# A transformer block's last stage: products in another order, operand sums made later, and all tokens written feature by feature

## The chip, the cores and the metric

The kernel runs on one core of one Trainium2 chip, in fp32 throughout. The metric is the device time of one execution in microseconds (us). Five engines work side by side, each through its own list of instructions in order: TensorE, shown as PE (matmuls) and PEld (loads of the stationary operand), VectorE (DVE), ScalarE (ACT), GpSimd (POOL) and SyncE (SP). DMAs are issued from an engine's list, here mostly SP's, and carried out by 16 DMA engines. An instruction that has to wait for another engine or for a transfer holds up everything behind it on its own engine.

## The reference

A block of a decoder with 1024 tokens and width 1024: a gated mixer of an mLSTM and of causal pools, then a SwiGLU layer of inner width 2816, then a last norm. The change touches the last two lines and nothing ahead of them.

```python
D_MODEL = 1024; SEQ = 1024; D_FF = 2816; EPS = 1e-6
def rms_norm(x, g):
    return x * lax.rsqrt(jnp.mean(x * x, axis=-1, keepdims=True) + EPS) * g
...
        x = x + (g_a * y_a + g_b * y_b) @ w_out[l]
        h2 = rms_norm(x, norm2_g[l])
        x = x + (jax.nn.silu(h2 @ w_ffn_gate[l]) * (h2 @ w_ffn_up[l])) @ w_ffn_down[l]
    return rms_norm(x, final_norm_g)
```

Inside the kernel most of it is held transposed: eight tiles of 128 features (`KT` = 8, `P` = 128), each with the tokens in a row.

## The kernel before, in words

**fp32 products.** A product of two fp32 blocks is three matmuls (`mm3`, lines 143 to 145): each operand is split into a high and a low part (`operand`, `split`: ACT casts the high part, line 131, DVE subtracts it for the low part, line 132), and high by high, high by low and low by high are summed in a PSUM bank of 128 x 512. `BANKS` gives 6 banks to "mm" and 2 to "aux".

**Seven products instead of eight.** The SwiGLU layer's last product, the *down stage*, treats the matrices as two by two blocks and gets the result from seven block products of sums, not eight. `OPS` names them b11, d1, d2, b21, d3, b22, d4. Their right operands (`tg`: hidden units by 512 tokens, high and low part side by side) were made in the gate/up stage ahead and lie in DRAM (`tg_d`). Their left operands (`a`) are made in the down stage from the four blocks of the weight: `a11`, `a12` (loaded into `raw`, `fh` = 0) and `a21`, `a22` (loaded into `rb`, `fh` = 1). b11 takes a11, b21 takes a12, d4 takes -a22; the other four take sums: s1 = a21 + a22 for d1, s1 - a11 for d2, a12 - (s1 - a11) for b22, a11 - a21 for d3.

**Loops.** The hidden units go in three chunks (`CHUNKS`: 4, 3 and 4 pairs of 128). In each chunk the seven steps of `STEPS` follow one another, and in each step the four column blocks `q` (`KH` = 4). One entry (c, s, q) is 12 matmuls of 512 columns (9 in the middle chunk) into one bank, and then DVE adds the bank to one half of a tile of `x` (the list `x3`, 8 tiles of 128 features x 1024 tokens, loaded at line 970 from the layer's input `x2_d`); this addition at line 1037 is called the eviction. In each half of the tiles are 512 tokens: the early ones (0 to 511) and the later ones.

**What is made ahead.** `down_rights` (line 938) queues a whole step's right operands on SP one step ahead; `tgp` has 13 places for them. `make_ready(e + EARLY)` makes the left operand of the entry four ahead. `down_lefts` is a generator that hands out a column's seven operands in the order of the steps; when d1's is asked for, it makes all four sums one after another (lines 920 to 924). The next chunk's weights are loaded in step three (`raw`) and step six (`rb`).

**Where the tiles lie.** The down stage's pools take the places that the gate/up stage's pools on the right side of SBUF had. In the order of their declaration (`s1p`, `rbp`, `tgp`, `ap`) they come to lie on that stage's operand tiles (in the trace `fb...`, `fd...`), and a first load into a place waits for the last matmul on the tile that lay there.

**The end.** In the last chunk finished features are squared and summed. The later 512 tokens are normed when d3 has come (`later_tokens`: a column of sums by four small matmuls, line 280; a power on POOL; the factor spread along a row by two matmuls on `diag`, line 273; one scaling for each of eight tiles, line 1004) and go out feature by feature as `out_0`. The early 512 tokens are turned into rows (`turn`: 28 transposes on PE, line 993, into `rows`), and the last entry runs in two halves of 256 tokens, each followed by its squares, its sum, its power, two transposes (line 1077), the scaling of whole rows by a number per partition (lines 1086 and 1088) and the output as `out_1` (line 1089).

The instructions on every engine are put in order by a scheduler that runs on a model of times, so the order in the program is not the code's.

Of the kernel before, what the change touches and what calls it, by code (L numbers as in the profile page):

```python
# [8 lines left out]
F32 = mybir.dt.float32  # L9
F32R = mybir.dt.float32r  # L10
# [37 lines left out]
EARLY = 4  # L48
# [18 lines left out]
def tile_hybrid_block(ctx, tc, x, xt, consts, params, w_fm, w_v, w_pool, w_a, w_b, w_out, w_gate, w_up, w_down, out, out_rows):  # L67
# [704 lines left out]
    with ExitStack() as c5:  # L772
# [121 lines left out]
        raws, lefts, rights, todo = {}, {}, {}, []  # L894
# [8 lines left out]
        def down_lefts(c, q):  # L903

            a11, a12 = raws[c, q, 0]
            n = a11.shape[-1]

            def tile_():
                t = ap.tile([P, 2, 512], F32R, tag="a", name="a")
                return t[:, :, :n]  # L910

            def op(src):
                t = tile_()
                operand(t, src)
# [5 lines left out]
            nc.vector.tensor_add(out=s1, in0=a21, in1=a22)  # L920
# [3 lines left out]
            nc.vector.tensor_sub(out=a12, in0=a12, in1=s1)  # L924
            yield t
            yield op(a12)
            yield op(a11)
            yield op(s1)
            yield op(a21)
            t = tile_()  # L930
            nc.scalar.activation(out=t[:, 0, :], in_=a22, func=AF.Copy, scale=-1.0)
            nc.vector.scalar_tensor_tensor(out=t[:, 1, :], in0=a22, scalar=-1.0, in1=t[:, 0, :].bitcast(F32), op0=ALU.mult, op1=ALU.subtract)
            yield t

        def down_rights(c, s):
            for i in range(*CHUNKS[c]):
                t = tgp.tile([P, 2, 512], F32R, tag="tg", name="tg")
                nc.sync.dma_start(out=t.bitcast(F32), in_=tg_d[i, OPS.index(STEPS[s])].rearrange("p (a n) -> p a n", a=2))
                rights.setdefault((c, s), []).append(t)

        entries = [(c, s, q) for c in range(len(CHUNKS)) for s in range(len(STEPS)) for q in range(KH)]

        def make_ready(e):
            if e >= len(entries):
                return
            c, s, q = entries[e]
            if s == 0:
                lefts[c, q] = down_lefts(c, q)
            todo.append(next(lefts[c, q]))
# [14 lines left out]
    op = pool(c7, "op", 4)  # L964
# [7 lines left out]
    rows = [op.tile([P, D], F32, tag="o", name="o") for _ in range(4)]  # L972
    LAST = KT - 1
    acc = [None, None]

    def square(j, half):

        sq = sqd.tile([P, 512], F32, tag=f"sq{half}", name="sq")
        nc.scalar.activation(out=sq, in_=halves(x3[j])[half], func=AF.Square)
        if acc[half] is not None:  # L980
            nc.vector.tensor_add(out=sq, in0=acc[half], in1=sq)
        acc[half] = sq

    def scaled(j):
        r = halves(x3[j])[0]
        nc.scalar.activation(out=r, in_=r, func=AF.Copy, scale=col(A_NF, j))

    def turn(t, j0, j1):

        ps = bank()  # L990
        n = (j1 - j0) * P
        for j in range(j0, j1):
            nc.tensor.transpose(out=ps[:, (j - j0) * P:(j - j0 + 1) * P], in_=x3[j][:, t * P:(t + 1) * P], identity=ident)  # L993
        copy = nc.scalar.copy if t % 2 else nc.vector.tensor_copy
        copy(out=rows[t][:, j0 * P:j1 * P], in_=ps[:, :n])

    def later_tokens():

        rs = sm.tile([P, 4], F32, tag="rs", name="rs3")
        inverse_rms(sm, token_sums(acc[1], 4), rs)  # L1000
        along_rows(sm, rsb2[0], rs, ap.tile([P, 2, 512], F32R, tag="a", name="diag"), 4)
        for j in range(KT):
            r = halves(x3[j])[1]
            nc.vector.scalar_tensor_tensor(out=r, in0=r, scalar=col(A_NF, j), in1=rsb2[0], op0=ALU.mult, op1=ALU.mult)  # L1004
            nc.sync.dma_start(out=out[j], in_=r)
# [5 lines left out]
    A, C = [None] * KH, [None] * KH  # L1011
    whole = slice(0, 512)
    for e, (c, s, q) in enumerate(entries):
        final = c == len(CHUNKS) - 1
        if q == 0:
            if s + 1 < len(STEPS):
# [8 lines left out]
        a, ts = todo.pop(0), rights[c, s]  # L1025
        (o10, o11), (o20, o21) = halves(x3[q]), halves(x3[q + KH])
        if final and s == 6 and q == KH - 1:
            break
        if s == 0:
            ps = bank()  # L1030
        elif s in (1, 2):
            ps = C[q] = bank() if s == 1 else C[q]
        else:
            ps = A[q] = bank() if s == 3 else A[q]
        product(ps, a, ts, whole, s in (0, 1, 3), True)
        o = (o10, o21, o11, o10, o11, o21, o20)[s]
        nc.vector.tensor_add(out=o, in0=ps, in1=o)  # L1037
        if not final:
            continue
        if s == 3:  # L1040
            square(q, 0)
            scaled(q)
        if s == 4:
            square(q, 1)
            if q == 1:
                for t in range(4):
                    turn(t, 0, KH)
        if s == 5:
            square(q + KH, 1)
            if q == KH - 1:  # L1050

                nc.vector.tensor_add(out=o20, in0=ps, in1=o20)
                later_tokens()
        if s == 6:
            square(q + KH, 0)
            scaled(q + KH)
    r, left, right = o20, a, ts
    sq = sqd.tile([P, 512], F32, tag="sq1", name="sq")
    ms = sm.tile([P, 4], F32, tag="ms", name="ms")
    rs = sm.tile([P, 4], F32, tag="rs", name="rs3")  # L1060
    for p in range(2):
        sl = slice(256 * p, 256 * (p + 1))
        two = slice(2 * p, 2 * p + 2)
        ps = bank()[:, :256]
        product(ps, left, right, sl, True, True)
        if p == 0:
            for t in range(4):
                turn(t, KH, LAST)
            nc.vector.tensor_scalar(out=ms, in0=token_sums(acc[0], 4), scalar1=1.0 / D, scalar2=EPS, op0=ALU.mult, op1=ALU.add)
        nc.vector.tensor_add(out=r[:, sl], in0=ps, in1=r[:, sl])  # L1070
        nc.scalar.activation(out=sq[:, sl], in_=r[:, sl], func=AF.Square)
        nc.vector.tensor_scalar_mul(out=r[:, sl], in0=r[:, sl], scalar1=col(A_NF, LAST))
        nc.vector.scalar_tensor_tensor(out=ms[:, two], in0=token_sums(sq[:, sl], 2), scalar=1.0 / D, in1=ms[:, two], op0=ALU.mult, op1=ALU.add)
        nc.gpsimd.tensor_tensor(out=rs[:, two], in0=ms[:, two], in1=nhalf[:, 0:2], op=ALU.pow)
        ps = bank("aux")
        for i in range(2):
            nc.tensor.transpose(out=ps[:, i * P:(i + 1) * P], in_=r[:, (2 * p + i) * P:(2 * p + i + 1) * P], identity=ident)
        for c0, c1 in ((0, 512), (512, D)):
            for i in range(2):
                t = 2 * p + i  # L1080
                sources = [(c0, min(c1, LAST * P), rows[t])] + [(LAST * P, D, ps)] * (c1 == D)
                for a, b, src in sources:
                    o = rows[t][:, a:b]
                    src = ps[:, i * P:(i + 1) * P] if src is ps else o
                    if i:
                        nc.scalar.activation(out=o, in_=src, func=AF.Copy, scale=rs[:, t:t + 1])
                    else:
                        nc.vector.tensor_scalar_mul(out=o, in0=src, scalar1=rs[:, t:t + 1])
                nc.sync.dma_start(out=out_rows[t * P:(t + 1) * P, c0:c1], in_=rows[t][:, c0:c1])
# [60 lines left out]
```

## Time and profile before

| | |
|---|---|
| time, median of 3 runs | 1507.25 us (1505.81 to 1508.13) |
| profiled execution: own time, span of the trace | 1509.98 us, 1508.3 us |
| mean granted TensorE clock | 0.99 of full speed |
| busy share of PE, PEld, DVE, ACT, POOL | 98%, 83%, 75%, 48%, 2% |
| DMA, mean over the span | 174 GB/s |

The span runs from the first to the last record of the trace; the execution's own time has 1.7 us more around it. A row of an engine's trace gives the start, the duration, the engine, the source line, the operation and its output and inputs by the program's names, then, in brackets, how long the engine had waited for what; `x8` is eight in a row. In rows of stretches come the length of the stretch, the busy time of PE, PEld, DVE, ACT and POOL (with their instructions), the granted clock, the DMA engines' share and GB/s.

### The profile page before, as it was taken

The numbers are of one execution on the slowest core, as the hardware profiler recorded it, in microseconds if no ns is written. First come the engines' busy times: TensorE is split into PE (matmuls) and PEld (weight loads), VectorE is DVE, ScalarE is ACT, GpSimd is POOL, SyncE is SP. The second block draws the span as 40 slices with busy tenths as digits, with TensorE's granted clock in tenths as the row PEclk, the third lists the DMA queues.
The fourth block names the chain that finished last, engine by engine and source line by source line (L and its number), as shares of the span: only waits on it lengthen the run. The fifth ranks groups of instructions, "written<-read, shape, count | busy, mean of one in ns | idle before, by whom it ended". The sixth has DMA issues, their size and how long they took to land.

```text
span 1508.3 us, 19546 instructions
## 1 busy us (share of the span) xinstructions
PE 1480.2 (98%) x7051; PEld 1249.0 (83%) x7051; DVE 1130.9 (75%) x2033; ACT 729.3 (48%) x1327; POOL 28.5 (2%) x58
## 2 busy tenths in 40 slices
PE   9999999999999999999999999999999998899996
PEld 9998888878887789998888788888888887788885
DVE  5757878797877678766567779888888876666765
ACT  6475655556543478862233455444444442222243
POOL 0000000000000011110000000000000000000000
PEclk9999999999999999999999999999999999899998
DMA  6662433233333598728343326434444446966633
GB/s 204 198 248 86 151 126 126 98 140 112 140 105 119 176 314 290 247 78 303 129 127 124 105 82 232 168 140 155 156 150 154 158 150 258 407 246 250 240 148 112
DMA packets 101296, 262.18 MB, mean 174 GB/s; under 512 B 9804, under 2 KB 45772, under 8 KB 101200
## 3 DMA queue, kind: packets, MB, share of 16 engines
q1 hardware_dynamic: 86032, 221.09, 42.0%
q10 hardware_dynamic: 15168, 39.85, 7.0%
q8 instruction: 55, 0.90, 0.3%
q14 instruction: 41, 0.34, 0.1%
HBM read 172.29 MB, written 88.62 MB: 173 GB/s over the span
## 4 chain that ended last, share of the span: by engine, by line
PE 95%; DVE 2%; DMA 1%; issue 1%; ACT 0%; SPq 0%; POOLq 0%; POOL 0%; ACTq 0%; DVEq 0%
PE mm L143 26%; PE mm L145 26%; PE mm L144 26%; PE mm L155 14%; DMA v<-v_d 1%; PE aux L683 0%; PE mm L524 0%; DMA yb<-yb_d 0%; DVE x L1004 0%; PE aux L573 0%; DMA o<-in_xt 0%; DVE a L132 0%; PE aux L280 0%; PE mm L993 0%; PE aux L143 0%
## 5 line engine op out<-in xcount | busy, mean ns | idle before, releaser
L131 ACT CAST s<-raw 128x512 fp32r<-128x512 f32 x220 | 133.6, 621 | 194.4 <-PE mm L145 158.7
L132 DVE TENSOR_TENSOR s<-raw,s 128x512 fp32r<-128x512 f32 x220 | 148.6, 686 | 29.6 <-ACT s L131 29.0
L143 PE MATMUL mm<-fd,s 128*128 128x512 f32 x352 | 137.6, 392 | 3.0 <-ACT e L226 2.2
L143 PE MATMUL mm<-zd,s 128*128 128x512 f32 x352 | 137.6, 393 | 0.3 <-DVE o L234 0.3
L144 PE MATMUL mm<-fd,s 128*128 128x512 f32 x352 | 137.6, 391 | 0.0
L145 PE MATMUL mm<-fd,s 128*128 128x512 f32 x352 | 137.5, 391 | 0.0
L145 PE MATMUL mm<-zd,s 128*128 128x512 f32 x352 | 137.5, 391 | 0.0
L144 PE MATMUL mm<-zd,s 128*128 128x512 f32 x352 | 137.3, 390 | 0.0
L143 PE MATMUL mm<-tg,a 128*128 128x512 f32 (+1 forms) x312 | 122.3, 392 | 7.4 <-ACT a L131 7.4
L144 PE MATMUL mm<-tg,a 128*128 128x512 f32 (+1 forms) x312 | 121.7, 390 | 0.0
L145 PE MATMUL mm<-tg,a 128*128 128x512 f32 (+1 forms) x312 | 121.6, 390 | 0.0
L1037 DVE TENSOR_TENSOR x<-mm,x 128x512 f32<-128x512 f32 x83 | 57.2, 689 | 63.0 <-PE mm L145 62.9
L143 PE MATMUL mm<-zb,s 128*128 128x512 f32 x264 | 104.0, 395 | 0.0
L143 PE MATMUL mm<-fb,s 128*128 128x512 f32 x264 | 103.0, 391 | 0.0
L144 PE MATMUL mm<-fb,s 128*128 128x512 f32 x264 | 103.0, 390 | 0.0
L144 PE MATMUL mm<-zb,s 128*128 128x512 f32 x264 | 102.9, 390 | 0.0
L145 PE MATMUL mm<-zb,s 128*128 128x512 f32 x264 | 102.9, 390 | 0.0
L145 PE MATMUL mm<-fb,s 128*128 128x512 f32 x264 | 102.7, 390 | 0.0
L143 PEld LDWEIGHTS mm<-fd,s 128*128 128x128 f32 x352 | 66.3, 188 | 17.8 <-ACT e L226 2.9
L143 PEld LDWEIGHTS mm<-zd,s 128*128 128x128 f32 x352 | 66.1, 188 | 14.7 <-DVE o L234 0.8
L145 PEld LDWEIGHTS mm<-fd,s 128*128 128x128 f32 x352 | 66.4, 189 | 13.9
L144 PEld LDWEIGHTS mm<-zd,s 128*128 128x128 f32 x352 | 66.1, 188 | 14.1 <-issue 0.5
(330 smaller groups left out, 3445.3 us busy)
## 6 DMA issues: line engine op xcount, KB each, us to landing
tg_d<-t SPq DMA_DIRECT2D x77, 512.0 KB, 3.4
tg<-tg_d SPq DMA_DIRECT2D x77, 512.0 KB, 6.0
raw<-in_w_fm SPq DMA_DIRECT2D x44, 512.0 KB, 3.7
z_d<-o ACTq DMA_DIRECT2D x24, 512.0 KB, 2.9
raw<-in_w_gate SPq DMA_DIRECT2D x22, 512.0 KB, 3.7
raw<-in_w_up SPq DMA_DIRECT2D x22, 512.0 KB, 4.6
q_d<-x ACTq DMA_DIRECT2D x16, 512.0 KB, 2.7
rc<-z_d SPq DMA_DIRECT2D x32, 256.0 KB, 5.2
```

The costliest lines, as they stand in the source:

```text
L131: hi_made = nc.scalar.copy(out=hi, in_=src)
L132: split.last = hi_made.ins, nc.vector.tensor_sub(out=lo, in0=src, in1=hi.bitcast(F32)).ins
L143: nc.tensor.matmul(out, lhsT=l[0], rhs=r[0], start=start, stop=False, skip_group_check=resume)
L144: nc.tensor.matmul(out, lhsT=l[0], rhs=r[1], start=False, stop=False, skip_group_check=resume)
L145: mm3.last = nc.tensor.matmul(out, lhsT=l[1], rhs=r[0], start=False, stop=stop, skip_group_check=resume)
L155: nc.tensor.matmul(ps[half], lhsT=l[a], rhs=r[half][b], start=(k == 0 and (a, b) == (0, 0)), stop=(k == nk - 1 and a == 1),)
L1037: nc.vector.tensor_add(out=o, in0=ps, in1=o)
```

## The change

Only the down stage changes.

- **Order of steps**: b21, b11, d1, b22, d2, d3, d4 in the first two chunks, and in the last one b11, d1, b22, d2, d3, d4 and b21 at the end. Before it was b21, d1, b22, b11, d2, d3, d4 in all three.
- **Sums with their operands**: `down_left` makes s1 at d1, s1 - a11 and a12 - (s1 - a11) at b22, a11 - a21 at d3. The sum for b22 goes to tiles of its own (`s4p`, two).
- **Ahead**: `EARLY` is 6, not 4. Both halves of the next weights are loaded in step d3. In d4 of the middle chunk the last chunk's operands for d4 and b21 are made, and kept in `apl` (8 tiles, where `rows` were).
- **Pools**: `tgp` 11 places, not 13, and ahead of `rbp`; `ap` 8, not 6. Banks of b21 and d1 for the first two columns come from "aux".
- **The end**: `last_norm(sl)` norms any run of tokens feature by feature, and its scaling reads the factor from PSUM. It is called for the later 512 tokens after d3, and for tokens 0 to 255 and 256 to 511 in the last step, b21, which runs over all four columns for the one and then for the other (so every quarter of tokens is of 256 columns, 48 matmuls each). Its outputs are issued by SP and ACT in turn. All tokens leave as `out_0`; `turn`, `rows`, `out_1` and the 28 + 4 transposes go.

```diff
-EARLY = 4
+EARLY = 6
...
         s1p = pool(c7, "s1p", KH, "right")
+        s4p = pool(c7, "s4p", 2, "right")
+        tgp = pool(c7, "tgp", 11, "right")
         rbp = pool(c7, "rbp", KH, "right")
-        tgp = pool(c7, "tgp", 13, "right")
-        ap = pool(c7, "ap", 6, "right")
-        STEPS = ("b21", "d1", "b22", "b11", "d2", "d3", "d4")
+        ap = pool(c7, "ap", EARLY + 2, "right")
+        STEPS = [("b21", "b11", "d1", "b22", "d2", "d3", "d4")] * 2 + [("b11", "d1", "b22", "d2", "d3", "d4", "b21")]
...
-            yield op(a12)
-            a21, a22 = raws[c, q, 1]
-            s1 = s1p.tile([P, 512], F32, tag="s1", name="s1")[:, :n]
-            nc.vector.tensor_add(out=s1, in0=a21, in1=a22)
-            t = op(s1)
-            nc.vector.tensor_sub(out=a21, in0=a11, in1=a21)
-            nc.vector.tensor_sub(out=s1, in0=s1, in1=a11)
-            nc.vector.tensor_sub(out=a12, in0=a12, in1=s1)
-            yield t
...
+            if b == "d1":
+                s1 = sums[c, q] = s1p.tile([P, 512], F32, tag="s1", name="s1")[:, :n]
+                nc.vector.tensor_add(out=s1, in0=a21, in1=a22)
+            elif b == "b22":
+                s1 = sums[c, q]
+                nc.vector.tensor_sub(out=s1, in0=s1, in1=a11)
+                s4 = s4p.tile([P, 512], F32, tag="s4", name="s4")[:, :n]
+                nc.vector.tensor_sub(out=s4, in0=a12, in1=s1)
+            elif b == "d3":
+                nc.vector.tensor_sub(out=a21, in0=a11, in1=a21)
+            operand(t, {"b21": a12, "b11": a11, "d1": sums.get((c, q)), "b22": b == "b22" and s4, "d2": sums.get((c, q)), "d3": a21}[b])
...
+    def last_norm(sl, sq):
+        n = sq.shape[-1] // P
+        rs = sm.tile([P, n], F32, tag="rs", name="rs3")
+        inverse_rms(sm, token_sums(sq, n), rs)
+        parts = [sm.tile([P, n], F32R, tag=f"rs{a}", name="rsp") for a in range(2)]
+        split(*parts, rs)
+        diag = ap.tile([P, 2, 512], F32R, tag="a", name="diag")
+        ps = bank("aux")[:, :n * P]
+        for a in range(2):
++            for t in range(n):
+                d, v = diag[:, a, t * P:(t + 1) * P], parts[a][:, t:t + 1].bitcast(F32)
+                if a:
+                    nc.vector.tensor_scalar_mul(out=d, in0=ident, scalar1=v)
+                else:
+                    nc.scalar.activation(out=d, in_=ident, func=AF.Copy, scale=v)
+            nc.tensor.matmul(ps, lhsT=ones_r, rhs=diag[:, a, :n * P], start=a == 0, stop=a == 1)
         for j in range(KT):
+            r = x3[j][:, sl]
+            nc.vector.scalar_tensor_tensor(out=r, in0=r, scalar=col(A_NF, j), in1=ps, op0=ALU.mult, op1=ALU.mult)
+            (nc.scalar if j % 2 else nc.sync).dma_start(out=out[j, :, sl], in_=r)
...
-        if s == 2 and not final:
-            down_weights(c + 1, q, 0)
-        if s == 5 and not final:
-            down_weights(c + 1, q, 1)
+        if c == 1 and b == "d4":
+            for last_s in (5, 6):
+                ahead[c + 1, last_s, q] = down_left(c + 1, last_s, q, apl)
+        if b == "d3" and not final:
+            for fh in range(2):
+                down_weights(c + 1, q, fh)
...
+    for sl in (slice(0, 256), slice(256, 512)):
+        for q in range(KH):
+            ps = bank()[:, :256]
+            product(ps, todo[q], ts, sl, True, True)
+            o = x3[q][:, sl]
+            nc.vector.tensor_add(out=o, in0=ps, in1=o)
+            square(q, sl)
+        last_norm(sl, sums_of(sl))
```

Three places in the program show how instructions move. First SP's list where the down stage begins. `tg` are right operands, `rb` weights, `x3` the tiles of `x`; in brackets stands what a DMA waits for, where `PE` is the last matmul on the tile that lay in its place, and `DMAHW` an earlier transfer of the same DMA lane. Before:

```order
L938 DMA tg_11265<-tg_d_91 128x1024 [waits DMAHW0_49,PE_49]
L938 DMA tg_11267<-tg_d_91 128x1024 [waits DMAHW1_49,PE_49]
L938 DMA tg_11269<-tg_d_91 128x1024 [waits DMAHW2_49]
L938 DMA tg_11271<-tg_d_91 128x1024 [waits DMAHW3_49,PE_49]
L900 DMA rb_11273<-in_w_down 128x1024 [waits DMAHW4_49]
L900 DMA rb_11275<-in_w_down 128x1024 [waits DMAHW5_49,PE_49]
L900 DMA rb_11277<-in_w_down 128x1024 [waits DMAHW6_49]
L900 DMA rb_11279<-in_w_down 128x1024 [waits DMAHW7_49]
```

After:

```order
L931 DMA tg_11268<-tg_d_91 128x1024 [waits DMAHW0_49,PE_49]
L931 DMA tg_11270<-tg_d_91 128x1024 [waits DMAHW1_49,PE_49]
L931 DMA tg_11272<-tg_d_91 128x1024 [waits DMAHW2_49]
L931 DMA tg_11274<-tg_d_91 128x1024 [waits DMAHW3_49]
L902 DMA rb_11276<-in_w_down 128x1024 [waits DMAHW4_49]
L902 DMA rb_11278<-in_w_down 128x1024 [waits DMAHW5_49]
L902 DMA rb_11280<-in_w_down 128x1024 [waits DMAHW6_49]
L902 DMA rb_11282<-in_w_down 128x1024 [waits DMAHW7_49]
```

The order is the same, and in both the eight `x3` loads and then the second step's four `tg` follow; what moved are the waits. The addresses say on which tiles the loads lie: before, the four `tg` on d1, b22, b22 and d3, and the second `rb` on d4; after, the first two `tg` on b21 and d4, the third on d4 too, and no `rb` waits for PE any more.

The second place is DVE's list in the middle chunk, where the last chunk's operands begin (`128x384` belongs to the middle chunk, `128x512` operands to the last; `x` rows at 1031 or 1037 are evictions). Before:

```order
L932 SCALAR_TENSOR_TENSOR a<-rb,a 128x384
L920 TENSOR_TENSOR s_12376<-rb 128x512
L922 TENSOR_TENSOR rb<-raw,rb 128x512
L1037 TENSOR_TENSOR x_11352<-mm,x_11352 128x512
L932 SCALAR_TENSOR_TENSOR a<-rb,a 128x384
L1037 TENSOR_TENSOR x_11354<-mm,x_11354 128x512
L132 TENSOR_TENSOR a<-raw,a 128x512
```

After:

```order
L913 SCALAR_TENSOR_TENSOR a<-rb,a 128x384
L917 TENSOR_TENSOR s_12368<-rb 128x512
L1031 TENSOR_TENSOR x_11355<-mm,x_11355 128x512
L913 SCALAR_TENSOR_TENSOR a<-rb,a 128x512
L924 TENSOR_TENSOR rb<-raw,rb 128x512
L132 TENSOR_TENSOR a<-raw,a 128x512
L913 SCALAR_TENSOR_TENSOR a<-rb,a 128x384
```

In both the first sum from the newly loaded `rb` (line 920, now 917) stands ahead of evictions and of operands that the middle chunk still needs; after the change it stands three evictions earlier, with two of d2 (`x_11355`, `x_11357`) and all four of d3 behind it, and the split for the last chunk's d4 (`a<-rb` of 512) comes in between.

The third is the end of PE's list. Before:

```order
L145 MATMUL mm<-tg,a 128x256
L273 MATMUL aux<-diag,ones_r 128x512
L280 MATMUL aux<-cst,sq 128x1 x4
L273 MATMUL aux<-diag,ones_r 128x512
L993 MATMUL mm<-cst,x_11354 128x128 x4
L280 MATMUL aux<-cst,sq 128x1 x2
L1077 MATMUL aux<-cst,x_11356 128x128 x2
L280 MATMUL aux<-cst,sq 128x1 x2
L1077 MATMUL aux<-cst,x_11356 128x128 x2
```

After:

```order
L145 MATMUL mm<-tg,a 128x256
L280 MATMUL aux<-cst,sq 128x1 x2
L992 MATMUL aux<-diag,ones_r 128x256
L280 MATMUL aux<-cst,sq 128x1 x2
L992 MATMUL aux<-diag,ones_r 128x256 x3
```

Behind the last product PE had the rest of the later tokens' norm, the last group of transposes and two short sums; now it has the sums of both runs of tokens and the four matmuls on `diag` that spread their factors.

More of the change, by code (lines that the diff above doesn't have):

```diff
@@ L66, in tile_hybrid_block @@
 @with_exitstack
[L67 removed]
+def tile_hybrid_block(ctx, tc, x, xt, consts, params, w_fm, w_v, w_pool, w_a, w_b, w_out, w_gate, w_up, w_down, out):
     nc = tc.nc
@@ L901, in down_weights, with down_left @@
             raws[c, q, fh] = t[:, :n], t[:, n:2 * n]
-        def down_lefts(c, q):
-            a11, a12 = raws[c, q, 0]
+        def down_left(c, s, q, pl=ap):
+            (a11, a12), (a21, a22) = (raws[c, q, fh] for fh in range(2))
             n = a11.shape[-1]
[L908 to L914, printed above, removed]
-                return t
-            yield op(a12)
-            a21, a22 = raws[c, q, 1]
-            s1 = s1p.tile([P, 512], F32, tag="s1", name="s1")[:, :n]
-            nc.vector.tensor_add(out=s1, in0=a21, in1=a22)
-            t = op(s1)
-            nc.vector.tensor_sub(out=a21, in0=a11, in1=a21)
-            nc.vector.tensor_sub(out=s1, in0=s1, in1=a11)
-            nc.vector.tensor_sub(out=a12, in0=a12, in1=s1)
-            yield t
[L926 to L933, printed above, removed]
@@ new lines, in down_left @@
+            b = STEPS[c][s]
+            t = pl.tile([P, 2, 512], F32R, tag="a", name="a")[:, :, :n]
+            if b == "d4":
+                nc.scalar.activation(out=t[:, 0, :], in_=a22, func=AF.Copy, scale=-1.0)
+                nc.vector.scalar_tensor_tensor(out=t[:, 1, :], in0=a22, scalar=-1.0, in1=t[:, 0, :].bitcast(F32), op0=ALU.mult, op1=ALU.subtract)
+                return t
+            if b == "d1":
[8 more added lines that the diff above has]
+                nc.vector.tensor_sub(out=a21, in0=a11, in1=a21)
@@ L937, in down_rights @@
                 t = tgp.tile([P, 2, 512], F32R, tag="tg", name="tg")
-                nc.sync.dma_start(out=t.bitcast(F32), in_=tg_d[i, OPS.index(STEPS[s])].rearrange("p (a n) -> p a n", a=2))
+                nc.sync.dma_start(out=t.bitcast(F32), in_=tg_d[i, OPS.index(STEPS[c][s])].rearrange("p (a n) -> p a n", a=2))
                 rights.setdefault((c, s), []).append(t)
-        entries = [(c, s, q) for c in range(len(CHUNKS)) for s in range(len(STEPS)) for q in range(KH)]
+        entries = [(c, s, q) for c in range(len(CHUNKS)) for s in range(len(OPS)) for q in range(KH)]
         def make_ready(e):
[L944 to L949, printed above, removed]
+            if e < len(entries):
+                todo.append(ahead.get(entries[e]) or down_left(*entries[e]))
         early_made = []
@@ L971, in tile_hybrid_block @@
         x3.append(t)
[L972 to L1001, printed above, removed]
+    acc = {}
@@ new lines, in square, with sums_of @@
+    def square(j, sl):
+        n = sl.stop - sl.start
+        sq = sqd.tile([P, n], F32, tag=f"sq{sl.start}-{n}", name="sq")
+        nc.scalar.activation(out=sq, in_=x3[j][:, sl], func=AF.Square)
+        key = sl.start, sl.stop
+        if key in acc:
+            nc.vector.tensor_add(out=sq, in0=acc[key], in1=sq)
+        acc[key] = sq
+    def sums_of(sl):
+        return acc[sl.start, sl.stop]
+    def last_norm(sl, sq):
[7 more added lines that the diff above has]
+        for a in range(2):
+            for t in range(n):
+                d, v = diag[:, a, t * P:(t + 1) * P], parts[a][:, t:t + 1].bitcast(F32)
[4 more added lines that the diff above has]
+            nc.tensor.matmul(ps, lhsT=ones_r, rhs=diag[:, a, :n * P], start=a == 0, stop=a == 1)
@@ L1009, in product @@
             mm3(ps, [a[:, i, kp * P:(kp + 1) * P] for i in range(2)], [t[:, i, sl] for i in range(2)], start and kp == 0, stop and kp == len(ts) - 1, True)
-    A, C = [None] * KH, [None] * KH
-    whole = slice(0, 512)
+    banks = {}
+    whole, later = slice(0, 512), slice(512, 1024)
     for e, (c, s, q) in enumerate(entries):
@@ L1020, in tile_hybrid_block @@
         make_ready(e + EARLY)
-        if s == 2 and not final:
-            down_weights(c + 1, q, 0)
-        if s == 5 and not final:
-            down_weights(c + 1, q, 1)
-        a, ts = todo.pop(0), rights[c, s]
+        b = STEPS[c][s]
+        if c == 1 and b == "d4":
[4 more added lines that the diff above has]
+                down_weights(c + 1, q, fh)
+        ts = rights[c, s]
         (o10, o11), (o20, o21) = halves(x3[q]), halves(x3[q + KH])
-        if final and s == 6 and q == KH - 1:
+        if final and b == "b21":
             break
[L1029 to L1032, printed above, removed]
-        else:
-            ps = A[q] = bank() if s == 3 else A[q]
-        product(ps, a, ts, whole, s in (0, 1, 3), True)
-        o = (o10, o21, o11, o10, o11, o21, o20)[s]
+        a = todo.pop(0)
+        if b in ("b21", "b11", "d1"):
+            ps = banks[b != "b11", q] = bank("aux" if b != "b11" and q < 2 else "mm")
+        else:
+            ps = banks[b == "b22", q]
+        product(ps, a, ts, whole, b in ("b21", "b11", "d1"), True)
+        o = {"b21": o10, "b11": o10, "d1": o21, "b22": o11, "d2": o11, "d3": o21, "d4": o20}[b]
         nc.vector.tensor_add(out=o, in0=ps, in1=o)
@@ L1039, in tile_hybrid_block @@
             continue
[L1040 to L1049, printed above, removed]
-            if q == KH - 1:
[L1052 to L1089, printed above, removed]
@@ new lines, in tile_hybrid_block @@
+        if b == "d2":
+            square(q, later)
+        if b == "d3":
+            square(q + KH, later)
+            if q == KH - 1:
+                last_norm(later, sums_of(later))
+        if b == "d4":
+            square(q + KH, whole)
+    for sl in (slice(0, 256), slice(256, 512)):
+        acc[sl.start, sl.stop] = acc[0, 512][:, sl]
+    for sl in (slice(0, 256), slice(256, 512)):
+        for q in range(KH):
[5 more added lines that the diff above has]
+        last_norm(sl, sums_of(sl))
```

16 lines of the change are left out of this document (6 added, 10 removed).

## The prediction

> **What bounds the kernel now.** I read the busy shares first, then what PE (TensorE's matmul side) waited for in the last 241 us, then PE, SyncE and the DMA engines around the one long wait, and last the closing 20 us.
>
> ```profile
> span 1508.3 us, 19546 instructions
> ...
> PE 1480.2 (98%) x7051; PEld 1249.0 (83%) x7051; DVE 1130.9 (75%) x2033; ACT 729.3 (48%) x1327; POOL 28.5 (2%) x58
> ```
>
> ```profile
> PE mm L143 <- ACT a L131: 7.4, 1, 7.4
> PE aux L280 <- DVE ms L1073: 5.5, 1, 5.5
> PE aux L1077 <- DVE ms L1073: 0.9, 1, 0.9
> ```
>
> PE is busy for 98% of the span. From 1267 us, where the down stage starts, it waits three times (who for whom, us, times, longest): once for 7.4 us inside the stage, and twice after its last product. So two places can pay, that wait and the end. Between them matmul follows matmul, and only PE's own work counts.
>
> PE around the long wait (start, duration, instruction), then SyncE's DMA issues, and one issue with its time to landing:
>
> ```profile
> 1265.87 0.39 PE L145 MATMUL mm<-fd,s 128*128 128x512 f32 x1
> ...
> 1267.46 0.39 PE L143 MATMUL mm<-tg,a 128*128 128x512 f32 x1
> ...
> 1278.11 0.39 PE L145 MATMUL mm<-tg,a 128*128 128x512 f32 x1
> 1285.94 0.77 PE L143 MATMUL mm<-tg,a 128*128 128x512 f32 x1 [7.44 <-ACT a L131]
> ...
> 1291.63 0.42 PE L144 MATMUL mm<-tg,a 128*128 128x512 f32 x1
> ```
>
> ```profile
> 1258.65 4.84 SPq L938 DMA_DIRECT2D tg<-tg_d  x4
> ...
> 1266.97 0.81 SPq L900 DMA_DIRECT2D rb<-in_w_down  x2
> ...
> 1268.31 6.33 SPq L970 DMA_DIRECT2D x<-x_d  x8
> 1275.60 2.88 SPq L938 DMA_DIRECT2D tg<-tg_d  x3
> ...
> tg<-tg_d SPq DMA_DIRECT2D x1, 512.0 KB, 10.2
> ```
>
> Step b21's 48 matmuls start from 1267.46 to 1278.11, 0.227 us apart. The next starts at 1285.94, and the 13 from there to 1291.63 take 5.7 us where 2.9 would do: the wait and the slow restart cost 7.4 + 2.8 = 10.2 us. The wait is put down to ACT, but I do not believe the name. The first matmul of d1 waits for its left operand and for its first right (`tg`):
>
> ```profile
> 1273.22 0.62 ACT L131 CAST a<-s 128x512 fp32r<-128x512 f32 x1 [0.84 <-DVE s L920]
> ...
> 1285.33 0.62 ACT L131 CAST a<-raw 128x512 fp32r<-128x512 f32 x1 [2.38 <-DVE raw L924]
> ```
>
> ```profile
> 1260.00:1267.00 7.00, 6.22 (x27) 4.81 (x26) 3.83 (x7) 0.61 (x2) 0.00 (x0) 1.00 1.01 367
> 1267.00:1269.00 2.00, 2.00 (x10) 1.68 (x9) 2.00 (x4) 0.62 (x2) 0.00 (x0) 1.00 0.71 188
> 1269.00:1286.00 17.00, 9.56 (x43) 7.61 (x42) 16.87 (x29) 4.86 (x8) 0.00 (x0) 0.87 1.03 405
> ```
>
> That operand, a cast from `s`, was there by 1273.84. The cast that ends at 1285.95 reads `raw` and belongs to b22, one step later. The first right of d1 was issued at 1275.60 and landed 10.2 us later, at 1285.8. In the stretches (busy us of PE, PEld, DVE, ACT, POOL, then granted clock, DMA share, GB/s) the DMA engines are full at 405 GB/s from 1269 to 1286. So bytes in the queue set this wait: d1's first right stands behind three remaining `rb` loads and eight `x` loads. DVE is full as well (16.87 of 17 us), but its work for d1 was ready.
>
> The end:
>
> ```profile
> 1487.38 0.28 PE L143 MATMUL mm<-tg,a 128*128 128x256 f32 x1
> ...
> 1487.50 0.28 PE L144 MATMUL mm<-tg,a 128*128 128x256 f32 x1
> ...
> 1490.99 0.28 PE L145 MATMUL mm<-tg,a 128*128 128x256 f32 x1
> ...
> 1491.10 0.39 PE L273 MATMUL aux<-diag,ones_r 128*128 128x512 f32 x1
> ...
> 1491.31 0.42 DVE L1070 TENSOR_TENSOR x<-mm,x 128x256 f32<-128x256 f32 x1 [0.17 <-PE mm L145]
> ...
> 1493.71 5.38 DVE L1004 SCALAR_TENSOR_TENSOR x<-x,par,rsb 128x512 f32<-128x512 f32 x8
> ...
> 1499.01 0.15 DVE L1073 SCALAR_TENSOR_TENSOR ms<-aux,ms 128x2 f32<-128x2 f32 x1
> 1499.21 1.01 PE L280 MATMUL aux<-cst,sq 128*128 128x1 f32 x4 [5.47 <-DVE ms L1073]
> 1499.23 0.69 POOL L1074 TENSOR_TENSOR rs<-ms,nhalf 128x2 f32<-128x2 f32 x1 [12.02 <-DVE ms L1073]
> ...
> 1503.05 0.34 ACT L1086 ACTIVATE o<-aux,rs 128x128 f32<-128x128 f32 x1
> ```
>
> ```profile
> 1504.34 0.59 SPq L1089 DMA_DIRECT2D out<-o  x1
> ```
>
> The last product ends at 1491.27 and the span 17.0 us later. In that time DVE first scales the later 512 tokens (5.38 us), with the last norm queued behind it, and the last DMA goes out 4.0 us before the end.
>
> **The change part by part.**
>
> *Where the loads of the stage's start wait: loses 4.4 us.* The down stage's pools lie on operand tiles of the gate/up stage. Before, the second right of b21 lay on `T["b22"][1]`; now it lies on `T["d4"][1]`, whose last reader is the matmul at 1265.87, nearly the end of that stage. Before, the matmul three later released an `rb` in the same way, and that went out at 1266.97. So the second right now goes out 3 x 0.227 earlier, at 1266.3, where all four rights were out by 1263.5. Behind it, in SyncE's order, come two more rights, four `rb`, eight `x`, and then the first right of the second step, now b11. That is the 16th transfer from 1266.3; before it was the 12th from 1266.97. One transfer of 512 KB takes 1.28 us of a full queue. The 12 took 1285.94 - 1266.97 = 18.97 us; 16 take 18.97 + 4 x 1.28 = 24.1, so PE goes on at 1290.4: +4.4 us. Least: the four fill the hole of 1267 to 1269 (0.71, 188 GB/s) and latency shrinks: +2.4. Most: all that moved from 1260 to 1267 at 367 GB/s moves again at the full rate: +6. I take the count. In b21 PE then also waits for the second right, 11 matmuls in, at 1269.95, for 1 to 2 us; the longer wait swallows that.
>
> By the Trainium skill (DMA: Bandwidth & Descriptors, Where 436 GB/s comes from), transfers between HBM and SBUF are bound on the HBM side, at about 358 GB/s. The 405 measured here speaks against it; at 358 the four transfers would make an estimated 5.9 us instead of 5.1, and the sum would be 0.8 us higher.
>
> *Step order, sums with their operands, EARLY 6, `ap` 8: 0.* With b11 second, four plain operands come before the first sum, and d1's sums are due a step (10.9 us) later. That takes work off DVE ahead of a wait that DVE does not set. After the restart a right lands every 1.28 us and feeds 12 matmuls (2.7 us), so the loads run ahead again. With 11 slots instead of 13 in `tgp` a right still goes out about a step before its use. The cover is that step; where loads come later than it, rival two begins.
>
> *Both halves of the next weights in step d3, and two steps' operands of the last chunk made ahead: 0, at most +5.*
>
> ```profile
> 1400.00:1410.00 10.00, 10.00 (x46) 8.27 (x45) 8.98 (x16) 3.12 (x5) 0.00 (x0) 1.00 0.87 331
> 1410.00:1420.00 10.00, 10.00 (x46) 8.29 (x45) 9.93 (x17) 2.34 (x4) 0.00 (x0) 1.00 0.44 160
> ```
>
> ```profile
> rb<-in_w_down SPq DMA_DIRECT2D x1, 512.0 KB, 6.0
> ```
>
> DVE now has the first sum from `rb` in its queue ahead of evictions of d2 and d3, and waits there for the load. Counted from the end of d2's first product in the middle chunk (t), `rb` goes out at t+1.6 and, by the 6.0 that such a load took from 1400 to 1402, lands at t+7.6. Sums, splits and evictions follow at 0.6 us each; the eviction that PE needs for d4's fourth product ends at about t+22, and PE gets there at t+24. PE's work covers it with 2 us to spare. That is why I take 0, and it is not much.
>
> *PE's own work: gains 1.8 us.* All 28 transposes go, 24 of them ahead of the last product's end, in three groups like this one of the chain that ended last:
>
> ```profile
> 1460.26 0.87 PE mm L993 x8
> ```
>
> 3 x 0.87 = 2.6 us. In the last step 36 more matmuls are split into 72 of 256 columns: 72 x 0.119 (1487.38 to 1487.50) - 36 x 0.227 = 0.4 more. The two matmuls on `diag` for the later tokens, after the last product before (1491.10), now stand ahead of it: 2 x 0.227 = 0.45. Together -1.75.
>
> *The end: gains 0.9 us.* Let E be the end of the last product. The later tokens' scaling now lies beside b21, from about E-9 to E-3.6; the addition that then frees a bank is out 1.1 us before PE wants the bank. But PE sums the first 256 tokens only after all products, and the two halves go through the long norm one after the other. My steps: last addition E+0.8; squares and their additions for both halves E+2.4; sums, power (0.69, as at 1499.23), split, diagonal blocks, and behind them the second half's sums, E+5.0; eight scalings to E+8.2; the second half's split and diagonals, queued behind those on DVE, E+9.2; eight scalings to E+12.5. One scaling is 0.40: 5.38/8, less the 0.27 by which 256 columns (L1070, 0.42) are shorter than 512 (L1037, 0.69, row below). The last DMA is half as large as before's, so I take 3.1 from its issue to the end: E+15.6. PE's small matmuls may be slow after idling (1.01 for four at 1499.21): E+16.1, against E+17.0. Ends: E+15.0, and E+18.5 if each hop costs 0.2 more.
>
> ```profile
> L1037 DVE TENSOR_TENSOR x<-mm,x 128x512 f32<-128x512 f32 x83 | 57.2, 689 | 63.0 <-PE mm L145 62.9
> ```
>
> Sum: 4.4 - 1.75 - 0.9 = **+1.7 us** on the profiled execution's own 1509.98 (its span and 1.7 around it). That stands 2.7 above the median of the runs, 1507.25; the same difference on the median gives **1509.0**.
>
> **Rivals.** A measurement of this kernel tells about 0.2% (3 us) from no change.
>
> One, faster: the wait is what the table says, operands that come late from DVE and ACT. Then b11 finds operands and right, and 10.2 us go besides: 1507.25 - 10.2 - 1.75 - 0.9 = 1494.4. For it: the name in the row, and a full DVE. Against: the cast named is another step's, and the right's landing meets the restart. 7%.
>
> Two, slower: DVE's new wait on `rb` in the middle chunk. From the point where `rb` lands over 8 us after its issue, evictions come later than PE wants their banks; with 10.2, as at the stage's start, PE waits 2 us and restarts slowly (2.8): 1509.0 + 5 = 1514. For it: both halves in one step, and DVE at 9.93 of 10 us there already. Against: the engines' share there was 0.44 to 0.87. The first term's upper end (+6) alone comes to 1510.6. Together 30%.
>
> Three, no change to be told: the late rights cost little, the hole at 1267 takes them up, and the end saves 2: 1507.25 + 2.4 - 1.75 - 2 = 1505.9. 12%.
>
> **Numbers.** The rest, 51%, is my forecast, with 1506 to 1512 as its own range. Slower: 26 of rival two's 30 and 6 from my forecast's upper edge, 0.32. Faster: rival one and 5 of the third's, 0.12. Same: 0.56. The range of 1504 to 1514 reaches the second rival and not the first; it leaves out rival one's 7, some 4 below 1504 and 9 above 1514.
>
> **What would show it.** After: SyncE issues the second `tg` at 1266.3; the DMA engines are full from 1268 to past 1290; PE's long wait ends at 1289 to 1292. If PE passes 1278 without one, rival one is right and I misread the releaser. A wait of PE over 1 us in 1380 to 1430 is rival two. No L993; the last product ends near 1493.9, the span 15 to 17 us later. What would make me wrong: another order of landing than the issues' order, or a tail whose hops cost more than the rows show.

## The result, and the profile after

The changed kernel takes 1509.74 us (median of 20 runs, 1507.88 to 1511.73), the kernel before 1507.95 us in as many runs: a ratio of 1.0014, 95% interval [1.0008, 1.0020], 1 to 3 us more. A second series gave 1.0006 [0.9997, 1.0016]. The forecast was 1509.0, no change to be told; it holds, and so do its two largest terms.

The page's head, what PE waited for from 1260 us on, and PE around the long wait, all of the changed kernel:

```profile
span 1507.4 us, 19555 instructions
PE 1475.2 (98%) x7051; PEld 1245.5 (83%) x7051; DVE 1133.0 (75%) x2053; ACT 718.0 (48%) x1314; POOL 28.9 (2%) x58
```

```profile
PE mm L143 <- DMA tg<-tg_d: 11.9, 1, 11.9
PE aux L992 <- DVE x L995: 2.1, 1, 2.1
PE aux L992 <- ACT diag L991: 2.1, 1, 2.1
PE aux L992 <- DVE diag L989: 1.2, 1, 1.2
...
```

```profile
1265.95 0.39 PE L145 MATMUL mm<-fd,s 128*128 128x512 f32 x1
1266.17 0.39 PE L143 MATMUL aux<-tg,a 128*128 128x512 f32 x1
...
1276.83 0.39 PE L145 MATMUL mm<-tg,a 128*128 128x512 f32 x1
1289.11 0.77 PE L143 MATMUL mm<-tg,a 128*128 128x512 f32 x1 [11.89 <-DMA tg<-tg_d]
...
1292.64 0.39 PE L145 MATMUL mm<-tg,a 128*128 128x512 f32 x1
```

The stage began 1.3 us earlier in this trace than in that of before (b21's first matmul at 1266.17, not 1267.46), so times are best counted from there. The wait stands where it stood, behind b21's 48 matmuls, and is 4.45 us longer (11.89 against 7.44). It is now put down to a right operand's DMA. The row of before named a cast of ACT for the same wait; the new name bears out the reading that this was not it.

SyncE's issues, one issue with its landing, and the stretches ahead of and in the wait:

```profile
1257.37 8.91 SPq L931 DMA_DIRECT2D tg<-tg_d  x4
1266.32 1.96 SPq L902 DMA_DIRECT2D rb<-in_w_down  x4
1268.33 9.46 SPq L959 DMA_DIRECT2D x<-x_d  x8
1278.74 11.88 SPq L931 DMA_DIRECT2D tg<-tg_d  x10
```

```profile
tg<-tg_d SPq DMA_DIRECT2D x1, 512.0 KB, 10.2
```

```profile
1260.00:1267.00 7.00, 6.22 (x28) 4.84 (x27) 4.97 (x9) 1.60 (x3) 0.00 (x0) 1.00 0.25 88
...
1269.00:1289.00 20.00, 8.21 (x37) 6.47 (x35) 18.07 (x31) 3.42 (x6) 0.00 (x0) 0.83 1.02 401
```

The four rights of b21 took SyncE 8.9 us to issue, where before it was 4.8: the second waited for its place. Ahead of 1267 us the DMA engines stood nearly idle, at 88 GB/s where they had moved 367: 279 GB/s x 7 us = 2.0 MB less, about four transfers of 512 KB. These four then move with the rest, at 401 GB/s and with the engines full. b11's first right, issued at 1278.74, lands 10.2 us later and lets PE go on.

The end, on PE and DVE:

```profile
1491.30 0.28 PE L145 MATMUL mm<-tg,a 128*128 128x256 f32 x1
1492.52 0.58 PE L280 MATMUL aux<-cst,sq 128*128 128x1 f32 x4 [0.94 <-DVE sq L970]
...
1495.56 0.85 PE L280 MATMUL aux<-cst,sq 128*128 128x1 f32 x4
```

```profile
1496.86 3.22 DVE L995 SCALAR_TENSOR_TENSOR x<-x,par,aux 128x256 f32<-128x256 f32 x8 [0.26 <-PE aux L992]
1500.00 0.15 DVE L132 TENSOR_TENSOR rsp<-rs,rsp 128x2 fp32r<-128x2 f32 x1
1500.19 0.48 DVE L989 TENSOR_SCALAR diag<-cst,rsp 128x128 fp32r<-128x128 f32 x2
1501.35 3.22 DVE L995 SCALAR_TENSOR_TENSOR x<-x,par,aux 128x256 f32<-128x256 f32 x8 [0.68 <-PE aux L992]
```

The last product ends at 1491.58, the span 15.8 us later (before: 17.0). The forecast had it near 1493.9; the earlier start of the stage and a shorter restart, below, make up the difference. Both runs' sums stand behind the last product, as the list of PE said.

### The profile page after: what moved, and what is told of

Its sections match the earlier page's. It is cut to its first block, busy times and chain, and to the rows that moved or that the text cites. A ratio compares the mean times of both kernels' runs of the same rounds, so it can differ in the third digit from the quotient of the medians.

```text
span 1507.4 us, 19555 instructions
## 1 busy us (share of the span) xinstructions
PE 1475.2 (98%) x7051; PEld 1245.5 (83%) x7051; DVE 1133.0 (75%) x2053; ACT 718.0 (48%) x1314; POOL 28.9 (2%) x58
## 4 chain that ended last, share of the span: by engine, by line
PE 94%; DMA 3%; DVE 1%; SPq 0%; ACT 0%; issue 0%; POOL 0%; DVEq 0%; ACTq 0%
PE mm L143 25%; PE mm L145 25%; PE mm L144 25%; PE mm L155 13%; PE aux L145 1%; PE aux L143 1%; PE aux L144 1%; DMA x<-x_d 1%; DMA tg<-tg_d 1%; PE mm L524 0%; PE aux L683 0%; DVE x L995 0%; DMA yb<-yb_d 0%; DMA q<-q_d 0%; DMA rc<-z_d 0%; DMA o<-in_xt 0%
## 5 line engine op out<-in xcount | busy, mean ns | idle before, releaser
L143 PE MATMUL mm<-tg,a 128*128 128x512 f32 (+1 forms) x266 | 100.6, 380 | 11.9 <-DMA tg<-tg_d 11.9
L144 PE MATMUL mm<-tg,a 128*128 128x512 f32 (+1 forms) x266 | 100.9, 379 | 0.0
L145 PE MATMUL mm<-tg,a 128*128 128x512 f32 (+1 forms) x266 | 100.2, 379 | 0.0
L1031 DVE TENSOR_TENSOR x<-mm,x 128x512 f32<-128x512 f32 x64 | 44.1, 690 | 49.9 <-PE mm L145 49.8
L143 PEld LDWEIGHTS mm<-fd,s 128*128 128x128 f32 x352 | 66.5, 189 | 17.9 <-ACT e L226 2.9
L143 PEld LDWEIGHTS mm<-zd,s 128*128 128x128 f32 x352 | 66.1, 188 | 14.7 <-DVE o L234 0.8
L145 PEld LDWEIGHTS mm<-fd,s 128*128 128x128 f32 x352 | 66.5, 189 | 13.9
L144 PEld LDWEIGHTS mm<-fd,s 128*128 128x128 f32 x352 | 66.4, 189 | 13.8
```

What stands on the lines that cost most here:

```text
L143: nc.tensor.matmul(out, lhsT=l[0], rhs=r[0], start=start, stop=False, skip_group_check=resume)
L144: nc.tensor.matmul(out, lhsT=l[0], rhs=r[1], start=False, stop=False, skip_group_check=resume)
L145: mm3.last = nc.tensor.matmul(out, lhsT=l[1], rhs=r[0], start=False, stop=stop, skip_group_check=resume)
```

## The experiments

Two theories were set against each other. *Queue*: PE's wait at the stage's start is the number of transfers ahead of the second step's first right, counted from the matmul that lets SyncE go on. *Operands*: it is work of ACT and DVE for the left operands, which the new order of steps and sums changes. The start of b21 lay between 1264.6 and 1268.3 us in the twelve traces, though no kernel changes anything ahead of the down stage's preparation; so the traces are compared from that start (in the version with the whole queue in order of use, 1.3 us of the 1268.3 are a wait ahead of it):

| kernel | PE's long waits in the stage | start of b21 to end of last product | from there to the end |
|---|---|---|---|
| before | 7.4 | 223.8 | 17.0 |
| changed | 11.9 | 225.4 | 15.8 |
| changed, second trace | 11.7 | 225.0 | 15.8 |
| changed, `rbp` ahead of `tgp` | 7.8 | 222.0 | 15.8 |
| before, `tgp` ahead of `rbp` | 12.4 | 228.0 | 17.0 |
| before, rights ahead of x | 2.0 and 0.5 | 218.3 | 17.0 |
| changed, rights ahead of x | 1.5 and 4.2 | 220.4 | 15.4 |
| changed, whole queue in order of use | none (1.3 ahead of it) | 211.8 | 15.8 |
| the same, b21's first right first | 0.3 | 212.2 | 15.8 |
| changed, one run at the end | 12.2 | 226.2 | 18.8 |
| changed, four entries ahead | 11.8 | 225.3 | 15.8 |
| changed, weights in two steps | 12.6 | 227.3 | 15.8 |

**The changed kernel again.**

> The changed kernel once more, for a second trace and as the base of the others. Queue theory: PE's only long wait in the stage is again 11 to 12.5 us, ahead of the first matmul of b11, put down to the landing of a right operand; time 1509.7. Rival (operands): the wait is of another length and follows an operand of ACT or DVE.

Measured: 1509.14 us, and a wait of 11.7 us for the same DMA. The base stands.

**The places alone, in the changed kernel.**

```diff
         s4p = pool(c7, "s4p", 2, "right")
+        rbp = pool(c7, "rbp", KH, "right")
         tgp = pool(c7, "tgp", 11, "right")
-        rbp = pool(c7, "rbp", KH, "right")
```

> The changed kernel with the pool of rb declared ahead of that of tg, as before the change; no step is moved. Queue theory: the second right is free early again and rb's second load waits instead, for the matmul that released the second right; b11's first right is then the 12th transfer after that matmul and not the 16th, so PE's wait falls from 11.9 by 4 x 1.28 = 5.1 to about 6.8 us, the restart costs 1 us more, and the time is 1505.5 (1504 to 1507). Rival (the loss comes with the order of the steps and the sums, the places are nothing): wait 11.9, time 1509.7.

Measured: 1505.60 us, ratio to the kernel before 0.9979 [0.9969, 0.9989]. What PE waited for, and SyncE's issues:

```profile
PE mm L143 <- DMA tg<-tg_d: 7.8, 1, 7.8
```

```profile
1255.79 5.32 SPq L931 DMA_DIRECT2D tg<-tg_d  x4
1261.17 3.55 SPq L902 DMA_DIRECT2D rb<-in_w_down  x4
```

The rights are out in 5.3 us again and the wait is shorter by 4.1 us, where 5.1 had been counted (7.8 us, not 6.8). Every step and sum is as in the changed kernel, so it is the places that cost it; with them back, the change as a whole gains 0.1 to 0.3%.

**The places alone, in the kernel before.**

```diff
-        rbp = pool(c7, "rbp", KH, "right")
         tgp = pool(c7, "tgp", 13, "right")
+        rbp = pool(c7, "rbp", KH, "right")
```

> The kernel before with the pool of tg declared ahead of that of rb (13 places, as before); nothing else. Queue theory: the second right waits for the matmul that released rb's second load, d1's first right becomes the 16th transfer after it, PE's wait grows from 7.4 by 5.1 to 12.5 us, the restart costs 1 us less: 1512 (1511 to 1513.5). Rival (places are nothing): 7.4 us and 1507.9.

Measured: 1514.38 us, ratio 1.0033 [1.0022, 1.0045], which is 3 to 7 us more; the wait is 12.4 us where 12.5 was forecast. The price in the wait is the same with the old order of steps. The median lies 0.9 us above the forecast's range of 1511 to 1513.5: in the traces b21's start to the last product is 4.2 us longer than before, and the six runs lie in two groups, at 1511 and at 1514 to 1515, for which no cause was found.

**The second step's rights ahead of x, in both kernels.** The edit in the kernel before (the other has the same):

```diff
+    down_rights(0, 1)
     x3 = []
...
-            if s + 1 < len(STEPS):
+            if (c, s) == (0, 0):
+                pass
+            elif s + 1 < len(STEPS):
                 down_rights(c, s + 1)
```

> The kernel before, with the four rights of its second step (d1) queued ahead of the eight x loads instead of behind them. Queue theory: d1's first right is the 4th transfer after 1266.97 instead of the 12th and lands before b21 ends; the wait of 7.4 goes, and the next step's first right, then the 16th, comes 1.8 us after PE wants it: 1507.9 - 10.2 + 1.8 + 1.7 for another restart = 1501 (1498 to 1503). Rival (operands from ACT and DVE set the wait, as the row before the change names it): a wait of 5 to 7 us stays ahead of d1, 1506 to 1508. Second rival: the x tiles, now later, hold DVE's evictions, and the wait moves to the third step at its old length: 1507.

Measured: 1503.20 us, ratio 0.9964 [0.9952, 0.9976], a little above the forecast's upper end. The wait of 7.4 us is gone, so bytes in the queue made it. What is left is not what I expected; PE's waits, and DVE at that time (L1040 is the eviction in this kernel):

```profile
PE mm L143 <- DVE x L1040: 2.5, 2, 2.0
```

```profile
1282.04 0.68 DVE L923 TENSOR_TENSOR s<-s,raw 128x512 f32<-128x512 f32 x1
1282.64 0.68 DVE L132 TENSOR_TENSOR a<-raw,a 128x512 fp32r<-128x512 f32 x1
1283.24 0.68 DVE L923 TENSOR_TENSOR s<-s,raw 128x512 f32<-128x512 f32 x1
1283.85 0.68 DVE L1040 TENSOR_TENSOR x<-mm,x 128x512 f32<-128x512 f32 x1
```

PE waits 2.0 us for a bank whose eviction is late. DVE never waits for an x tile there (no brackets); the eviction stands behind sums and splits, 0.60 us each. The sum of line 923 is d2's and leads to b22's: the old order makes all four sums as soon as d1 asks for them. With rights on time, DVE's work is the next limit of the old order, and the second rival (x tiles hold DVE) is wrong. The clock of PE fell behind this wait, which the last section takes up.

> The changed kernel, with the four rights of its second step (b11) queued ahead of the eight x loads: the same edit that was made to the kernel before. Queue theory: b11's first right is the 8th transfer after the late second right and not the 16th, and lands 12.7 us after b21 starts, which lasts 10.9: a wait of 1.8 us; d1's first right comes behind the x loads, 4 transfers later than b11's first came, at 28.1, and PE wants it at 24.6: a wait of 3.5. With two short restarts (2) 7.3 us instead of 11.9 + 1.7: 1503 (1500 to 1505). Rival (the step order or the operands set the wait): one wait of 8 us or more stays ahead of b11, 1508 to 1509.5.

Measured: 1503.72 us, ratio 0.9973 [0.9962, 0.9983]. The two waits:

```profile
1277.39 0.47 PE L143 MATMUL mm<-tg,a 128*128 128x512 f32 x1 [1.45 <-DMA tg<-tg_d]
```

```profile
1292.74 0.76 PE L143 MATMUL aux<-tg,a 128*128 128x512 f32 x1 [4.19 <-ACT a L131]
```

PE goes on 12.5 and 27.8 us after b21's start; the count of transfers gave 12.7 and 28.1. The second wait is again put down to ACT. The fourth of d1's casts, the cast that ended just ahead of PE, and the issue of d1's first right at 1282.38 with its landing:

```profile
1279.39 0.62 ACT L131 CAST a<-s 128x512 fp32r<-128x512 f32 x1 [2.39 <-DVE s L917]
...
1292.00 1.22 ACT L131 CAST a<-s 128x512 fp32r<-128x512 f32 x2 [4.10 <-DVE s L922]
```

```profile
tg<-tg_d SPq DMA_DIRECT2D x1, 512.0 KB, 10.2
```

d1's operands, from the sums of line 917, were all cast by 1280.01. The casts at 1292.00 read the sum of line 922 and belong to b22, one step later, as in the trace of before. d1's first right lands at 1292.6, and PE starts at 1292.74. So I take the landing for the releaser here too; in the next version, where d1's rights go out earlier, this wait is gone.

**The queue in the order of use.** In the changed kernel `rb` is loaded ahead of b21's rights, then come the rights of b21 and b11, four x tiles, the rights of d1, and the other four:

```diff
+        for q in range(KH):
+            down_weights(0, q, 1)
         down_rights(0, 0)
-        for q in range(KH):
-            down_weights(0, q, 1)
...
-                nc.sync.dma_start(out=t.bitcast(F32), in_=tg_d[i, OPS.index(STEPS[c][s])].rearrange("p (a n) -> p a n", a=2))
+                down_rights.last = nc.sync.dma_start(out=t.bitcast(F32), in_=tg_d[i, OPS.index(STEPS[c][s])].rearrange("p (a n) -> p a n", a=2))
...
+    down_rights(0, 1)
     x3 = []
     for j in range(KT):
+        if j == KH:
+            down_rights(0, 2)
         t = x3p.tile([P, S], F32, tag="x3", name="x3")
-        nc.sync.dma_start(out=t, in_=x2_d[j])
+        with tc.issue_after(down_rights.last.ins):
+            nc.sync.dma_start(out=t, in_=x2_d[j])
...
-            if s + 1 < len(OPS):
+            if (c, s) in ((0, 0), (0, 1)):
+                pass
+            elif s + 1 < len(OPS):
```

> The changed kernel with another order in SyncE's queue alone: the four rb ahead of the rights of b21, then the rights of b21 and b11, four x tiles, the rights of d1, the other four x tiles. Queue theory: every right lands before its step begins (b11's first at 7.6 us after b21's start against 10.9, d1's first at 17.8 against 21.8), so wait and restart of 13.6 us go: 1509.4 - 13.6 = 1496 (1495 to 1499; the upper end if evictions wait for x tiles, as they did for 2.5 us in the kernel before with its rights ahead). Rival (DVE, busy for 18 of the 20 us there, has not made d1's operands in time): PE waits 5 us or more for an operand ahead of d1, 1501 or more.

Measured: 1495.97 us, ratio 0.9924 [0.9912, 0.9937], the fastest version here together with the next one. Its stretch and PE's one wait for a right:

```profile
1268.00:1290.00 22.00, 21.68 (x96) 17.95 (x97) 21.80 (x37) 4.47 (x8) 0.00 (x0) 1.00 1.02 406
```

```profile
PE aux L143 <- DMA tg<-tg_d: 1.3, 1, 1.3
```

PE is busy for 21.68 of 22 us (8.21 of 20 in the changed kernel), at full clock, with the DMA engines as full as before. DVE is busy for 21.80 of 22, and PE does not wait for it. The forecast's first rival, operands that come late, falls here, and so does the operands theory. The evictions that I feared for the upper end did not hold PE.

The 1.3 us stand ahead of b21, whose first right was now behind the `rb`. One more version puts it first (the four `rb` are queued inside `down_rights`, after its first load):

> As the version with rb first, x tiles in two groups of four and all rights ahead of their steps, but with the first right of b21 ahead of the four rb. Queue theory: in that version b21's first right came 1.3 us late behind the rb; now it is out early, and the second right lands as in the changed kernel without a wait: 1496 - 1.3 to 1.6 = 1494.5 (1493.5 to 1496). Rival (the late matmul that releases the second right, or DVE at full load, sets the start of the stage): 1496.

Measured: 1496.21 us, ratio 0.9924 [0.9910, 0.9938]. In the trace the wait is 0.3 us, 3.2 us into b21, instead of 1.3 ahead of it; in the time nothing is to be seen; the intervals of both are 2 us to each side, so whether the 1 us is gained stays open. The time is the rival's 1496 and lies just above the forecast's range.

**The end in one run.**

```diff
-    for sl in (slice(0, 256), slice(256, 512)):
-        acc[sl.start, sl.stop] = acc[0, 512][:, sl]
-    for sl in (slice(0, 256), slice(256, 512)):
+    for sl in (slice(0, 512),):
         for q in range(KH):
-            ps = bank()[:, :256]
+            ps = bank()[:, :512]
```

> The changed kernel with the last step's 512 tokens in one run of 512 columns instead of two of 256. By the forecast's steps: PE 0.4 us less; squares, sums and diagonal blocks are twice as long, so the first scaling starts 6.9 us after the last product instead of 5.3, eight scalings of 0.67 end at 12.3, the last, larger DMA at 15.9: no change within 0.5 us, 1509 (1508 to 1511). Rival (the two runs hide the first half's norm under the second half's products): 3 us slower, 1512.5.

Measured: 1512.16 us, ratio 1.0025 [1.0016, 1.0034]. I was wrong, and the rival's time came out. The chain behind the last product, on PE and DVE:

```profile
1496.66 1.84 PE L280 MATMUL aux<-cst,sq 128*128 128x1 f32 x8 [4.25 <-DVE sq L970]
1501.37 1.22 PE L992 MATMUL aux<-diag,ones_r 128*128 128x512 f32 x2 [2.87 <-ACT diag L991]
```

```profile
1502.63 5.36 DVE L995 SCALAR_TENSOR_TENSOR x<-x,par,aux 128x512 f32<-128x512 f32 x8 [1.52 <-PE aux L992]
```

The last product ends at 1492.41. The sums start 4.25 us later, since squares on ACT and their additions on DVE wait for each other in turn; the sums take 1.84 us and POOL's power 1.0. Scaling begins 10.2 us after the last product, not 6.9. In the changed kernel it begins at 5.3: the first run's squares lie under the second run's products, its sums do not.

**Four entries ahead, and the weights in two steps.**

```diff
-EARLY = 6
+EARLY = 4
```

> The changed kernel with operands made four entries ahead instead of six (and two places fewer in their pool, which lies behind all others, so that no other tile moves). Forecast: nothing, 1509.4, since PE's only long wait is for a right. Rival (the longer lead carries part of the result): new waits of PE for operands or for banks, 1511 or more.

```diff
-        if b == "d3" and not final:
-            for fh in range(2):
-                down_weights(c + 1, q, fh)
+        if b in ("b22", "d3") and not final:
+            down_weights(c + 1, q, int(b == "d3"))
```

> The changed kernel with the two halves of the next weights loaded in steps b22 and d3, one in each, instead of both in d3. Forecast: nothing, 1509.4, since DVE's waits for rb in the first and middle chunk (4.5 us in three) do not reach PE. Rival two of the prediction (the load of both halves at once costs PE time): faster by 1 us or more, 1508 or less.

Measured: 1509.64 us, ratio 1.0018 [1.0008, 1.0029], and 1509.45 us, ratio 1.0011 [1.0002, 1.0020]. Next to the changed kernel's 1509.1 to 1509.7 both do nothing, as forecast: no wait of PE but the one for b11's right and the usual ones at the end.

## Why the prediction was right

- **Loads at the stage's start, +4.4.** Measured 4.45 in the first trace and 4.3 in the second, and undone or brought about by the order of two pools alone. Counted from b21's start, the second right does go out 3 matmuls sooner than the `rb` of before (at 1265.01, 1.16 us ahead of it, against 0.49), and the 16 transfers from there to PE's next matmul take 24.1 us, as summed. One detail was wrong: PE was to wait 1 to 2 us for b21's second right, and did not. I had overlooked that the same late issue leaves the DMA engines idle ahead of it (0.25 busy, 88 GB/s), so that it lands 3.2 us after its issue, half a microsecond before PE wants it.
- **The restart.** The sum took it as equal on both sides. In the trace of before 13 matmuls were some 0.43 us apart, in that of the changed kernel 8, and in the six other traces with this wait 7 to 14. That is worth 1.1 us in this pair of traces, which from b21's start on differ by 0.4 us, less than the medians do. Traces of the changed kernel with edits far behind this wait spread as widely, so I put it down to chance (see the last section). That the price is equal on the median is not measured; the sum below agrees with it.
- **PE's own work, -1.75.** From b21's start to the last product, without waits, before took 216.4 us. Less its restart of 2.8 that is 213.6. The changed kernel, less its wait of 11.9 and its restart of 1.7, takes 211.8, and so does the version without any long wait: -1.8.
- **The end, -0.9.** 17.0 to 15.8: -1.2, a third more than summed. The last scalings end 13.0 us after the last product where I had 12.5, and from there to the end it is 2.8 us, where I took 3.1.
- **Step order, sums, lead: 0.** True as the kernel stands. Once the rights are on time it is not: with its second rights ahead of x the old order waits 2.5 us for DVE, and the new one with the same edit does not, nor with the whole queue in order. What the change gains there was hidden behind the queue. (The old order was not run with the whole queue in order of use.)
- **Both halves of the weights in d3: 0.** DVE did wait for `rb`, as the second rival said, and PE did not. Of the three waits below one, of 1.9 us, stands at the stage's start; the middle chunk's is the longest, 2.2 us:

```profile
DVE s L917 <- DMA rb<-in_w_down: 4.5, 3, 2.2
```

```profile
1400.00:1410.00 10.00, 10.00 (x46) 8.29 (x45) 10.00 (x18) 5.44 (x11) 0.00 (x0) 1.00 0.92 335
1410.00:1420.00 10.00, 10.00 (x45) 8.28 (x45) 10.00 (x18) 1.87 (x3) 0.00 (x0) 1.00 0.38 124
```

- **Rivals.** The first fell with the queue in the order of use. The second fell already in the changed kernel's trace, which has no wait of PE from 1380 to 1430, and with the weights in two steps. The third, no loss from the late rights, is ruled out by the two kernels that differ in the order of pools alone.

The sum, 4.4 - 1.8 - 1.2 = +1.4 us, is what the medians show: +1.8 in the first series, +0.9 in the second. The forecast of +1.7 had the right terms; that it lies so close to the first series is partly luck, since the end was off by 0.3 and the two series differ by 0.9.

## What to carry to other kernels

Where one engine issues loads in order, the first load whose place is still in use holds all behind it; so the order of pool declarations, which decides what lies on what, can cost more than a rewritten stage gains. Queue loads in the order in which they are wanted, and count the transfers ahead of each step: here that alone was worth about 13 us. When a wait's named releaser had another step's work to do, look for a transfer that lands at the same moment.

## What the runs showed of the hardware

PE's slow restart is its granted clock, which steps between full and half. Inside the stage every stretch at half is a multiple of 3.41 us long: 10.24 in the traces of before and of the changed kernel, 13.65 in two others, 6.83 after the wait of 4.2 us. After the wait of 1.45 us no slow matmul came. After that of 2.0 us, in the kernel before with its rights ahead of x, the clock was full at first and then fell, with PE back at work; the stretch that holds the wait, and the one behind it:

```profile
1281.98:1285.40 3.42, 1.42 (x7) 0.91 (x6) 3.42 (x7) 0.79 (x2) 0.00 (x0) 1.00 1.03 392
1285.40:1288.81 3.41, 3.41 (x9) 2.64 (x8) 3.41 (x7) 1.07 (x2) 0.00 (x0) 0.50 1.02 414
```

After waits of 4.2 us and more the clock was already at half when PE went on. The first matmul took 0.76 or 0.77 us, and the next ones stayed 0.43 us apart until the stretch ended, 2.9 to 6.0 us after the restart. Each wait of 4.2 us and more so cost 1.4 to 2.9 us more than its length, and the wait of 2.0 us cost 1.7 more. The Trainium skill (TensorE: Matmul & The Clock Gate, Part 1) has the clock go down after an idle window of about 3.4 us and up after a busy one, with windows that run free of the kernel. The traces agree with the length of the windows and with their running free: PE's cost depends on where in a window it goes on, which accounts for the spread. One of them shows besides that a window need not be idle throughout: here PE was busy for 1.42 us of the 3.42.

A core alone moved 401 to 406 GB/s for 20 us in loads from HBM, so the bound of about 358 GB/s that the prediction weighed (the Trainium skill, DMA: Bandwidth & Descriptors, Where 436 GB/s comes from) did not hold here: 512 KB took 1.28 us, not 1.46.
